# Two-layer encoder trunk: another order of loads, warming products and norm sums at the program's begin

## Chip, cores and metric

The kernel runs on one core of one Trainium2 chip. The metric is the device time of one execution in microseconds (us), lower is better. A number such as L652 is a line of the kernel before. Engines are named as in the profile: PE does the matrix products, ACT and DVE the elementwise work, POOL a few fills, SP issues most of the transfers, and a DMA can also be issued from ACT's queue.

## The reference, cut to what matters

Input x is 512 positions by 1024 channels, in float32. Each of the two layers is this:

```python
hn = rmsnorm(x, norm_mix_g[l])
proj = hn @ w_in[l]
(aq, ak, av, bx, by, cq, ck, cv, dq, dk, dv, gl) = jnp.split(proj, split_points, axis=-1)
ya = mixer_a(aq, ak, av, ...)            # dense attention
yb = mixer_b(bx, by, conv_w[l], ...)     # convolution, two gated scans over time, GeLU gate
yc, yd = mixer_c(cq, ck, cv, ...), mixer_d(dq, dk, dv, ...)   # windowed attentions
merged = sum(gate_i * (y_i @ w_proj_i))
x = x + merged @ w_out[l]
x = x + jnp.square(jax.nn.relu(rmsnorm(x, norm_mlp_g[l]) @ w_mlp1[l])) @ w_mlp2[l]
```

A last rmsnorm follows. rmsnorm scales each position by 1/sqrt(mean of squares + eps). In mixer_b the scan's decay is `a = exp(log_a)` and its input is `sqrt(1 - a*a) * (i * xc)`; r and i are sigmoids of small products of xc, the output of the convolution of bx.

## The kernel before, in words

**Products.** Channels lie on the 128 partitions, positions along the free axis. A float32 product is done as three: every operand is split into a high part (a cast, on ACT) and a low part (a subtraction, on DVE), and PE multiplies high by high, high by low and low by high. Weights come in chunks of 128 by 1024 (eight tiles of 128 columns; `PLAN` lists their order). A chunk is loaded by SP (`wload`, L96), cast by ACT (`whi`, L111, three buffers) and subtracted by DVE (`wlo`, L122); `take` (L147) hands the next one out and casts up to three chunks ahead. The cast of a chunk waits until PE has done with the chunk three places earlier. A group of products over one chunk is 24 products, three for each of eight k.

**The begin.** `setup` (L294) loads the vectors `ve`, fills `ones` on DVE and copies one element of it on ACT. `all` (L1379) issues 16 products of `ones` by `ones`, whose result nobody reads, then loads the eight x tiles and the first chunks on SP. `xg_tile` (L247) makes the high part xh of an x tile times the norm's gain on ACT and the low part xl on DVE; `sumsq` (L255) adds up squares for the norm, whose factor is applied later. Chunks 0 and 1 come in halves.

**Phase 1 of a layer** (`phase1`, L417) runs the 30 groups of `P1SEQ` (L47) in this order; n is the place in it: BX0 and BX1 (n = 0, 1) interleaved by `several`, K0, K1, BX2 (n = 4), AQ, AQ, BX3, BY0 and so on, then pairs of groups for CQ0, CQ1, DQ0, DK0 (n = 20, 21), DQ1 (22, 23), DK1 (24, 25), DQ2, DK2. After each pair `rope` rotates its two results on DVE. `norm_cols` (L264) makes the norm's factor from the squares with eight small products, `rows` and `spread_rows` turn it into a tile `rb` that `conv_b` (L577) and others multiply by.

**The queue of small steps.** The steps of mixer_b are not issued where their data come up but put in a queue `bq`. `conv_b` adds three steps (tap 0 on ACT, taps 1 and 2, tap 3 on DVE) and, for its first two tiles, a split; `gelu_b` three; `gates_b` (L631) does four small groups of three products, one tanh on ACT each (L652), and adds for its tile f: s1 twice (three activations on ACT, L661 to L663), s2 twice (two operations on DVE, L669 and L670), s3 (two square roots on ACT, L675), s4 twice (a product and a scan on DVE, L679 and L681), s5 (two operations on DVE, L685 and L686, then a cast on ACT, L687) and s6 (DVE, L690). After group n as many steps are taken from the queue as `TICKS[n]` (L49) says, fewer if it holds fewer. `gates_b` is called after the groups 16, 18, 24 and 25 for f = 0 to 3. Before its own products it empties the queue as far as it needs to:

```python
while self.bq and (f not in self.xch or (f > 1 and f - 2 not in self.bdone)):
    self.tick(1)
```

where `bdone` gets f in step s6. So `gates_b(3)`, after group 25, takes steps until s6 of f = 1 is out. Engines work in the order of issue.

**Accumulators.** `wide` (L165) hands out accumulator tiles by the tags mm, s and t in turn, two buffers for each tag; a buffer is free again when its last reader in the program is done. Group 24 has tag mm and is read by the rope after group 25. The four tiles of `gates_b(2)` have the tags s, t, mm, s, group 25 has t, and the tiles of `gates_b(3)` have mm, s, t, mm.

Nothing reorders any of this: the program's order is the order on each engine.

Of the kernel before, what the change touches and what calls it, by code (L numbers as in the profile page):

```python
# [11 lines left out]
F32 = mybir.dt.float32  # L12
F32R = mybir.dt.float32r
I32 = mybir.dt.int32
AF = mybir.ActivationFunctionType
ALU = mybir.AluOpType
# [7 lines left out]
KD = DM // 128  # L24
# [17 lines left out]

E1, E2, E3, FN = (2, 5, 2, 16)

WU, P0, P1 = (16, 2, 2)

P1SEQ = [("BX", 0), ("BX", 1), ("K", 0), ("K", 1), ("BX", 2), ("AQ", 0, 0), ("AQ", 0, 1), ("BX", 3), ("BY", 0),  # L47
         ("AQ", 1, 0), ("AQ", 1, 1), ("BY", 1), ("BY", 2), ("BY", 3)] + [k + (z,) for k in QKS for z in range(2)]
# [27 lines left out]
class Body:  # L76
# [19 lines left out]
    def wload(self):  # L96
        i = self.n_load
        if i >= len(self.order):
            return
        raw = self.rawp.tile([128, 1024], F32, tag="raw", name="raw")  # L100
        for s in self.parts(i):
            self.nc.sync.dma_start(out=raw[:, s], in_=self.w[i][:, s])
        self.raws[i] = raw
        self.n_load += 1

    def parts(self, i):

        n = (P0, P1, 1)[min(i, 2)]
        return [slice(p * (1024 // n), (p + 1) * (1024 // n)) for p in range(n)]

    def whi(self):  # L111
        i = self.n_split
        while self.n_load <= i:
            self.wload()
        hi = self.hlp.tile([128, 1024], F32R, tag="whi", name="whi")
        lo = self.hlp.tile([128, 1024], F32R, tag="wlo", name="wlo")
        for s in self.parts(i):
            self.nc.scalar.copy(hi[:, s], self.raws[i][:, s])  # L118
        self.hls[i] = (hi, lo)
        self.n_split += 1  # L120

    def wlo(self):  # L122
        i = self.n_lo
        hi, lo = self.hls[i]
        raw = self.raws.pop(i)
        for s in self.parts(i):
            self.nc.vector.tensor_tensor(out=lo[:, s], in0=raw[:, s], in1=hi[:, s].bitcast(F32), op=ALU.subtract)  # L127
        self.n_lo += 1

    def ahead(self, i):  # L130
# [143 lines left out]
    def rows(self, cols, n, pool):  # L274

        nc, rw = self.nc, self.rw
        nc.vector.tensor_copy(rw[:, :, 0:n].bitcast(F32R), cols)
        nc.vector.tensor_tensor(out=rw[:, :, 32:32 + n], in0=cols, in1=rw[:, :, 0:n], op=ALU.subtract)
        ps = self.misc()
        m = 32 + n  # L280
        for c in range(4):
            nc.tensor.matmul(ps[0:m, c * 128:(c + 1) * 128], rw[:, c, 0:m], self.ident)
        row = pool.tile([m, S], F32R, tag=f"row{n}", name="row", bufs=1)
        nc.scalar.copy(row, ps[0:m, :])
        return row
# [8 lines left out]
    def setup(self):  # L294
        nc = self.nc
        cp = self.cp
        self.cs = cp.tile([128, NC_], F32, name="cs")
        self.ve = cp.tile([128, DEPTH * NV + 8], F32, name="ve")
        self.ones = cp.tile([128, 128], F32, name="ones")
        nc.sync.dma_start(out=self.ve, in_=self.vec)  # L300
        nc.vector.memset(self.ones, 1.0)
        nc.scalar.copy(self.ones[0:1, 0:1], self.ones[0:1, 0:1])
        self.ident = self.cs[:, C_ID:C_ID + 128]
        nl = DEPTH
        self.xh = self.xgp.tile([128, KD, S], F32R, name="xh")
        self.xl = self.xgp.tile([128, KD, S], F32R, name="xl")
        self.acc = cp.tile([128, S], F32, name="acc")
        self.rb = cp.tile([128, S], F32, name="rb")
        self.d_hb = cp.tile([128, nl, 32], F32, name="d_hb")
        self.d_lgb = cp.tile([128, nl, 16], F32, name="d_lgb")  # L310
        self.d_sp = cp.tile([128, nl, 8], F32, name="d_sp")
        self.d_nsp = cp.tile([128, nl, 8], F32, name="d_nsp")
        self.d_nsink = cp.tile([128, nl, 8], F32, name="d_nsink")
# [103 lines left out]
    def phase1(self, l):  # L417
        nc, p1 = self.nc, self.p1
        nv, ns = nc.vector, nc.scalar
# [23 lines left out]
        X, sqt, SUM = {}, {}, {}  # L443
# [3 lines left out]
        def squares(key, Xs, n=128):  # L447

            sqt[key] = []
            for z, x in enumerate(Xs):  # L450
                if z == 0 or n == 128:
                    sq = p1.tile([128, S], F32, tag="sqq", name="sqq", bufs=2)
                    sqt[key].append(sq)
                    o = 0
                else:
                    o = n
                ns.activation(out=sq[o:o + n], in_=x[0:n], func=AF.Square)
# [29 lines left out]


        X["bx", 0], X["bx", 1] = self.several([("BX", f) for f in range(2)], self.xmv, (1, 2, 3, 4, 6))
        rcol = self.rcol = self.norm_cols()  # L490
        nv.tensor_scalar(out=self.rs8, in0=rcol, scalar1=0.125, scalar2=None, op0=ALU.mult)
        nv.tensor_scalar(out=self.nrs8, in0=rcol, scalar1=-0.125, scalar2=None, op0=ALU.mult)
        r2 = self.smt(4, "r2")
        nv.tensor_tensor(out=r2, in0=rcol, in1=rcol, op=ALU.mult)
        X["k", 0] = self.group("K", 0)
        row = self.rows(rows(rcol, 1), 1, p1)
        X["k", 1] = self.group("K", 1)
        ns.copy(self.rb, self.spread_rows(row, 1, 0))
        if l == 0:
            self.derive()  # L500

        rd = self.drp.tile([S], F32, tag="rd", name="rd")
        nc.sync.dma_start(out=rd.rearrange("(c p) -> p c", p=128), in_=rcol)
        nc.sync.dma_start(out=self.roff, in_=rd.rearrange("(p r) -> p r", r=4))
        self.conv_b(l, 0, X["bx", 0])
        self.conv_b(l, 1, X["bx", 1])
        squares("k", (X["k", 0], X["k", 1]), 64)
        X["bx", 2] = self.group("BX", 2)
        self.conv_b(l, 2, X["bx", 2])
        head_sums("k", 2, C_SELK)  # L510
        yk = head_scale("k", 2)
# [867 lines left out]
    def all(self):  # L1379
        nc = self.nc  # L1380
        self.setup()
        self.xs = self.drp.tile([KD, 128, S], F32, tag="xs", name="xs")
        warm = self.misc()
        with self.tc.tile_pool(name="xin", bufs=1) as xin:
            self.sqp = xin
            xt = xin.tile([128, KD, S], F32, name="xt")
            for _ in range(WU):
                nc.tensor.matmul(warm[:, 0:128], self.ones, self.ones)
            xg = lambda c: self.xg_tile(xt[:, c], c, self.v(0, V_GMIX + c))
            for c in range(KD):  # L1390
                nc.sync.dma_start(out=xt[:, c], in_=self.x[c])
                if c in (0, 1, KD - 1):
                    self.wload()
            nc.sync.dma_start(out=self.cs, in_=self.cst)
            for c in range(KD):
                xg(c)
                if c < 2:
                    self.whi()
                    self.lows()
                if c >= 2:  # L1400
                    self.sumsq(xt[:, c - 2], c == 2)
            for c in range(KD - 2, KD):
                self.sumsq(xt[:, c], False)
        for l in range(DEPTH):
            self.layer(l)
# [10 lines left out]
def _pack_weights(i):  # L1416
# [13 lines left out]
    for l in range(DEPTH):  # L1430
# [3 lines left out]
        for key in PLAN:  # L1434
# [36 lines left out]
            else:  # L1471
                c = cols(i["w_mlp2"][l][a[0] * DM:(a[0] + 1) * DM], span(0, a[1]))
            parts.append(np.ascontiguousarray(c).reshape(128, 1024))
    return np.stack(parts)


# [77 lines left out]
```

## Time and profile before

| | before |
|---|---|
| median of 3 runs | 2004.0 us (2003.87 to 2004.54) |
| the profiled execution's own time | 2003.11 us |
| its span in the profile | 2001.3 us |
| PE busy | 1984.2 us, 99% of the span |
| DVE, ACT busy | 1299.9 us (65%), 1000.5 us (50%) |

Times in the profile count from the start of the span. In a timeline a row is: start in us, duration in us, engine, line, operation, written tile <- read tiles, shapes, how many were merged into the row, and in brackets the idle time of the engine before it and what ended it. PEld is the load of weights that goes ahead of a product. A float32 product of `ones` shows as two records.

### The profile page before, as it was taken

To read this page: it belongs to the slowest core of one execution; us is meant where nothing else is said; L and a number is where in the kernel's file an instruction comes from. 1 tells how busy PE (TensorE), PEld (TensorE's weight loads), DVE (VectorE), ACT (ScalarE), POOL (GpSimd) and SP (SyncE) were. 2 spreads that over 40 slices of the span, in tenths; PEclk is the share of its full clock that TensorE was granted. 3 is DMA by queue.
4 is the path that set the end of the run, shared out by engine and by line. 5 is a ranking of instruction groups with operands and counts; after the bars stand their busy time and mean duration, and the time that the engine had idled before them with its cause. 6 is when DMAs were issued, how large, how long until landed. Compare 5 with 4: busy or idle time off the path is not lost.

```text
span 2001.3 us, 25982 instructions
## 1 busy us (share of the span) xinstructions
PE 1984.2 (99%) x9732; PEld 1654.7 (83%) x9732; DVE 1299.9 (65%) x2330; ACT 1000.5 (50%) x1751; POOL 1.7 (0%) x12
## 2 busy tenths in 40 slices
PE   9999999999999999999999999999999999999998
PEld 7888789888888888888888888898877888888887
DVE  6889775766666554444658897758675755544445
ACT  4357786855734332332333668868466344332322
POOL 0000000000000000000000000000000000000000
PEclk9999999999999999999999999999999999999999
DMA  5544415334443223323335553152343423323231
GB/s 194 159 145 141 134 54 154 116 101 116 117 131 131 94 97 95 101 90 104 123 111 169 157 167 97 53 172 93 111 131 95 162 95 105 95 95 103 91 102 64
DMA packets 92910, 233.35 MB, mean 117 GB/s; under 512 B 17496, under 2 KB 23768, under 8 KB 92784
## 3 DMA queue, kind: packets, MB, share of 16 engines
q1 hardware_dynamic: 89904, 227.50, 36.7%
q10 hardware_dynamic: 2880, 4.20, 0.6%
q8 instruction: 77, 1.26, 0.3%
q14 instruction: 49, 0.40, 0.1%
HBM read 207.38 MB, written 24.27 MB: 116 GB/s over the span
## 4 chain that ended last, share of the span: by engine, by line
PE 88%; DVE 7%; ACT 3%; issue 2%; DMA 1%; SPq 0%; DVEq 0%; ACTq 0%
PE ps_mm L177 12%; PE ps_mm L179 12%; PE ps_mm L178 11%; PE ps_t L177 6%; PE ps_t L179 6%; PE ps_t L178 6%; PE ps_s L177 6%; PE ps_s L179 6%; PE ps_s L178 6%; PE ps_o L890 2%; PE ps_t L869 2%; DVE wlo L127 1%; ACT whi L118 1%; PE ps_s L830 1%; PE ps_s L980 1%
## 5 line engine op out<-in xcount | busy, mean ns | idle before, releaser
L118 ACT CAST whi<-raw 128x1024 fp32r<-128x1024 f32 (+1 forms) x318 | 329.0, 1041 | 310.5 <-PE ps_mm L178 99.6
L127 DVE TENSOR_TENSOR wlo<-raw,whi 128x1024 fp32r<-128x1024 f32 (+1 forms) x318 | 384.6, 1213 | 89.5 <-ACT whi L118 86.5
L177 PE MATMUL ps_mm<-xh,whi 128*128 128x512 f32 x720 | 285.9, 397 | 0.2
L179 PE MATMUL ps_mm<-xh,wlo 128*128 128x512 f32 x720 | 281.2, 391 | 1.1 <-DVE wlo L127 1.1
L178 PE MATMUL ps_mm<-xl,whi 128*128 128x512 f32 x720 | 280.9, 390 | 0.0
L179 PEld LDWEIGHTS ps_mm<-xh,wlo 128*128 128x128 f32 x720 | 135.2, 188 | 31.4 <-DVE wlo L127 1.9
L177 PEld LDWEIGHTS ps_mm<-xh,whi 128*128 128x128 f32 x720 | 135.3, 188 | 27.8 <-ACT whi L118 1.1
L178 PEld LDWEIGHTS ps_mm<-xl,whi 128*128 128x128 f32 x720 | 135.4, 188 | 26.2
L177 PE MATMUL ps_t<-xh,whi 128*128 128x512 f32 x368 | 143.8, 391 | 0.0
L179 PE MATMUL ps_t<-xh,wlo 128*128 128x512 f32 x368 | 143.2, 389 | 0.0
L178 PE MATMUL ps_t<-xl,whi 128*128 128x512 f32 x368 | 143.2, 389 | 0.0
L177 PE MATMUL ps_s<-xh,whi 128*128 128x512 f32 x352 | 138.7, 394 | 0.0
L179 PE MATMUL ps_s<-xh,wlo 128*128 128x512 f32 x352 | 137.1, 389 | 0.0
L178 PE MATMUL ps_s<-xl,whi 128*128 128x512 f32 x352 | 137.0, 389 | 0.0
L879 DVE TENSOR_TENSOR PT<-ps_t,PT 128x512 fp32r<-128x512 f32 (+2 forms) x128 | 75.0, 586 | 63.4 <-ACT PT L876 58.9
L863 ACT ACTIVATE P<-P,al 128x512 f32<-128x512 f32 (+2 forms) x128 | 82.7, 646 | 18.9 <-DVE al L862 17.8
L876 ACT CAST PT<-ps_t 128x512 fp32r<-128x512 f32 (+2 forms) x128 | 63.8, 500 | 46.2 <-PE ps_o L890 42.7
L177 PEld LDWEIGHTS ps_t<-xh,whi 128*128 128x128 f32 x368 | 69.1, 188 | 15.1 <-issue 1.0
L179 PEld LDWEIGHTS ps_t<-xh,wlo 128*128 128x128 f32 x368 | 69.1, 188 | 14.5
L178 PEld LDWEIGHTS ps_t<-xl,whi 128*128 128x128 f32 x368 | 69.1, 188 | 14.2
L177 PEld LDWEIGHTS ps_s<-xh,whi 128*128 128x128 f32 x352 | 66.1, 188 | 14.6 <-issue 1.3
L178 PEld LDWEIGHTS ps_s<-xl,whi 128*128 128x128 f32 x352 | 66.1, 188 | 14.0 <-issue 0.5
(434 smaller groups left out, 4184.9 us busy)
## 6 DMA issues: line engine op xcount, KB each, us to landing
raw<-in_w_dram SPq DMA_DIRECT2D x314, 512.0 KB, 3.5
Qr<-qD SPq DMA_DIRECT2D x48, 128.0 KB, 3.9
Kd<-kD SPq DMA_DIRECT2D x48, 128.0 KB, 3.9
qsA<-stk SPq DMA_DIRECT2D x32, 128.0 KB, 2.3
qsC<-stk SPq DMA_DIRECT2D x32, 128.0 KB, 2.5
K<-ks SPq DMA_DIRECT2D x16, 256.0 KB, 8.7
Q<-qsA SPq DMA_DIRECT2D x16, 256.0 KB, 6.3
Q<-qsC SPq DMA_DIRECT2D x16, 256.0 KB, 5.6
```

What stands on the lines that cost most here:

```text
L118: self.nc.scalar.copy(hi[:, s], self.raws[i][:, s])
L127: self.nc.vector.tensor_tensor(out=lo[:, s], in0=raw[:, s], in1=hi[:, s].bitcast(F32), op=ALU.subtract)
L177: mm(ps, sh, mh, start=(k == 0), stop=False)
L178: mm(ps, sh, ml, start=False, stop=False)
L179: mm(ps, sl, mh, start=False, stop=(k == n - 1))
L830: nc.tensor.matmul(ps[:, 0:n], qq, Kt[j][:, 0, b0 * 128:b1 * 128], start=True, stop=False)
L863: ns.activation(out=P[:, 0:n], in_=P[:, 0:n], func=AF.Copy, scale=ls)
L869: nc.tensor.transpose(pt[:, b * 128:(b + 1) * 128], P[:, b * 128:(b + 1) * 128], self.ident)
L876: ns.copy(st["dst"][0], st["src"])
L879: nv.tensor_tensor(out=st["dst"][1], in0=st["src"], in1=st["dst"][0].bitcast(F32), op=ALU.subtract)
L890: nc.tensor.matmul(o, a, b, start=(n_ == 0), stop=(n_ == len(mm) - 1))
L980: nc.tensor.matmul(ps[:, o:o + w], Q[:, q0:q0 + 128], K[:, z, k0:k0 + w], start=(z == 0), stop=(z == 1))
```

## The change

At the begin, the warming products go from 16 to 11 and no longer wait for ACT's copy of an element of `ones` (that copy now has another target and comes later). `ve` is loaded from ACT's queue. Chunks 0 and 1 come in four quarters each: the first quarters from ACT's queue, the others from SP between the x tiles; casts and subtractions of a quarter come after every second x tile. The squares of the x tiles start after the sixth tile in place of the third, and chunk 2 is split before the last five of them.

In phase 1 of both layers, `norm_cols` comes after K0 (before: ahead of it), `rows` after K1 (before: after K0), `spread_rows` and `rb` in the middle of BX2 (before: after K1), the squares of K ahead of BX2, and the `conv_b` of the tiles 0 and 1 after BX2 (before: ahead of it). `P1SEQ`, `TICKS` and `GATES` are as before.

```diff
-WU, P0, P1 = (16, 2, 2)
+WU, P0 = (11, 4)
...
-        raw = self.rawp.tile([128, 1024], F32, tag="raw", name="raw")
-        for s in self.parts(i):
-            self.nc.sync.dma_start(out=raw[:, s], in_=self.w[i][:, s])
-        self.raws[i] = raw
+        raw = self.raws[i] = self.rawp.tile([128, 1024], F32, tag="raw", name="raw")
+        self.nc.sync.dma_start(out=raw, in_=self.w[i])
...
+    def first_loads(self, queue, p):
+
+        s = slice(p * (1024 // P0), (p + 1) * (1024 // P0))
+        for i in range(2):
+            if p == 0:
+                self.raws[i] = self.rawp.tile([128, 1024], F32, tag="raw", name="raw")
+            queue.dma_start(out=self.raws[i][:, s], in_=self.w[i][:, s])
+        self.n_load = 2
+
+    def first_split(self, p):
+        s = slice(p * (1024 // P0), (p + 1) * (1024 // P0))
+        for i in range(2):
+            if p == 0:
+                self.hls[i] = [self.hlp.tile([128, 1024], F32R, tag=t, name=t) for t in ("whi", "wlo")]
+            hi, lo = self.hls[i]
+            self.nc.scalar.copy(hi[:, s], self.raws[i][:, s])
+            self.nc.vector.tensor_tensor(
+                out=lo[:, s], in0=self.raws[i][:, s], in1=hi[:, s].bitcast(F32), op=ALU.subtract
+            )
...
-        nc.sync.dma_start(out=self.ve, in_=self.vec)
+        nc.scalar.dma_start(out=self.ve, in_=self.vec)
         nc.vector.memset(self.ones, 1.0)
-        nc.scalar.copy(self.ones[0:1, 0:1], self.ones[0:1, 0:1])
...
         X["bx", 0], X["bx", 1] = self.several([("BX", f) for f in range(2)], self.xmv, (1, 2, 3, 4, 6))
+        X["k", 0] = self.group("K", 0)
         rcol = self.rcol = self.norm_cols()
...
-        X["k", 0] = self.group("K", 0)
+        X["k", 1] = self.group("K", 1)
         row = self.rows(rows(rcol, 1), 1, p1)
-        X["k", 1] = self.group("K", 1)
-        ns.copy(self.rb, self.spread_rows(row, 1, 0))
         if l == 0:
             self.derive()
...
+        squares("k", (X["k", 0], X["k", 1]), 64)
+        X["bx", 2] = self.group("BX", 2, within=lambda: ns.copy(self.rb, self.spread_rows(row, 1, 0)))
         self.conv_b(l, 0, X["bx", 0])
         self.conv_b(l, 1, X["bx", 1])
-        squares("k", (X["k", 0], X["k", 1]), 64)
-        X["bx", 2] = self.group("BX", 2)
         self.conv_b(l, 2, X["bx", 2])
...
+            load = lambda c: nc.sync.dma_start(out=xt[:, c], in_=self.x[c])
+            load(0)
+            self.first_loads(nc.scalar, 0)
+            nc.scalar.copy(self.d_sp[0:1, 0, 0:1], self.ones[0:1, 0:1])
+            for p in range(P0):
+                if p > 0:
+                    self.first_loads(nc.sync, p)
+                for c in (2 * p + 1, 2 * p + 2):
+                    if c < KD:
+                        load(c)
+            self.wload()
+            nc.sync.dma_start(out=self.cs, in_=self.cst)
             xg = lambda c: self.xg_tile(xt[:, c], c, self.v(0, V_GMIX + c))
             for c in range(KD):
-                nc.sync.dma_start(out=xt[:, c], in_=self.x[c])
-                if c in (0, 1, KD - 1):
-                    self.wload()
-            nc.sync.dma_start(out=self.cs, in_=self.cst)
-            for c in range(KD):
                 xg(c)
-                if c < 2:
-                    self.whi()
-                    self.lows()
-                if c >= 2:
-                    self.sumsq(xt[:, c - 2], c == 2)
-            for c in range(KD - 2, KD):
+                if c % 2 == 0:
+                    self.first_split(c // 2)
+                if c >= 5:
+                    self.sumsq(xt[:, c - 5], c == 5)
+            self.whi()
+            self.lows()
+            for c in range(3, KD):
                 self.sumsq(xt[:, c], False)
```

## Rows read from the trace of the kernel before

**Rows 1.** The page, part 1: busy time, share of the span, instructions of each engine.

```profile
PE 1984.2 (99%) x9732; PEld 1654.7 (83%) x9732; DVE 1299.9 (65%) x2330; ACT 1000.5 (50%) x1751; POOL 1.7 (0%) x12
```

**Rows 2.** Waits of PE: total us, times, longest; the two longest lines of eight.

```profile
PE ps_misc L1388 <- ACT ones L302: 2.3, 1, 2.3
PE ps_s L1340 <- ACT dg L1336: 1.7, 1, 1.7
```

**Rows 3.** Timeline of the begin, all engines.

```profile
0.74 1.28 ACT L302 ACT_TABLE_LOAD   x1 [0.74 <-PEq L1546]
0.84 0.17 DVE L301 MEMSET ones<- 128x128 f32 x1 [0.84 <-PEq L1546]
...
2.28 6.03 PE L1388 MATMUL ps_misc<-ones 128*128 128x128 f32 x32 [2.28 <-ACT ones L302]
...
3.95 0.72 ACT L250 ACTIVATE xh<-xt,ve 128x512 fp32r<-128x512 f32 x1 [1.72 <-DMA xt<-in_x_dram]
...
7.22 0.72 ACT L250 ACTIVATE xh<-xt,ve 128x512 fp32r<-128x512 f32 x1 [0.20 <-DMA xt<-in_x_dram]
...
8.06 0.47 PE L206 MATMUL ps_s<-xh,whi 128*128 128x512 f32 x1
...
19.03 0.39 PE L208 MATMUL ps_t<-xh,wlo 128*128 128x512 f32 x1
```

**Rows 4.** Warming products by stretch: length, PE busy (records), granted clock, DMA share, GB/s.

```profile
2.28:6.28 4.00, 4.00 (x18) 1.00 0.89 283
7.28:7.78 0.50, 0.50 (x7) 1.00 1.05 369
```

**Rows 5.** Timeline of PE, layer 0: gates of tiles 2 and 3.

```profile
159.28 0.39 PE L177 MATMUL ps_s<-xch,whi 128*128 128x512 f32 x1
...
167.44 0.39 PE L177 MATMUL ps_mm<-xch,whi 128*128 128x512 f32 x1
...
169.48 0.39 PE L177 MATMUL ps_mm<-xch,whi 128*128 128x512 f32 x1
```

**Rows 6.** Timeline of ACT in the same stretch.

```profile
148.41 1.06 ACT L118 CAST whi<-raw 128x1024 fp32r<-128x1024 f32 x1 [0.18 <-ACT whi L118]
...
151.30 0.82 ACT L661 ACTIVATE btq<-btg,d_sp 128x512 f32<-128x512 f32 x1
...
156.53 1.28 ACT L675 ACT_TABLE_LOAD   x1
...
161.02 0.63 ACT L675 ACTIVATE btq<-btq 128x512 f32<-128x512 f32 x1 [2.56 <-DVE btq L669]
...
163.90 0.69 ACT L652 ACTIVATE btg<-ps_s,d_lgb 128x512 f32<-128x512 f32 x1
...
167.92 0.62 ACT L687 CAST yB<-btq 128x512 fp32r<-128x512 f32 x1 [1.59 <-DVE btq L686]
168.44 0.68 ACT L652 ACTIVATE btg<-ps_mm,d_lgb 128x512 f32<-128x512 f32 x1
```

**Rows 7.** Timeline of DVE in the same stretch.

```profile
158.34 2.04 DVE L378 TENSOR_TENSOR stkf<-tt 128x512 f32<-128x512 f32 x2
160.30 0.68 DVE L669 SCALAR_TENSOR_TENSOR btq<-btg,btq 128x512 f32<-128x512 f32 x1
...
162.22 1.22 DVE L681 TENSOR_TENSOR_SCAN btq<-bta,btg 128x512 f32<-128x512 f32 x1
163.37 1.20 DVE L127 TENSOR_TENSOR wlo<-raw,whi 128x1024 fp32r<-128x1024 f32 x1
...
167.19 0.69 DVE L686 SCALAR_TENSOR_TENSOR btq<-btq,yb 128x512 f32<-128x512 f32 x1
```

**Rows 8.** Timeline of ACT and PE, layer 1, the same place.

```profile
1157.41 0.62 ACT L687 CAST yB<-btq 128x512 fp32r<-128x512 f32 x1 [1.58 <-DVE btq L686]
1157.94 0.68 ACT L652 ACTIVATE btg<-ps_mm,d_lgb 128x512 f32<-128x512 f32 x1
...
1158.98 0.39 PE L177 MATMUL ps_mm<-xch,whi 128*128 128x512 f32 x1
```

More of the change, by code (lines that the diff above doesn't have):

```diff
@@ L99, in wload @@
             return
-        raw = self.rawp.tile([128, 1024], F32, tag="raw", name="raw")
-        for s in self.parts(i):
-            self.nc.sync.dma_start(out=raw[:, s], in_=self.w[i][:, s])
-        self.raws[i] = raw
+        raw = self.raws[i] = self.rawp.tile([128, 1024], F32, tag="raw", name="raw")
+        self.nc.sync.dma_start(out=raw, in_=self.w[i])
         self.n_load += 1
-    def parts(self, i):
-        n = (P0, P1, 1)[min(i, 2)]
-        return [slice(p * (1024 // n), (p + 1) * (1024 // n)) for p in range(n)]
+    def first_loads(self, queue, p):
[15 more added lines that the diff above has]
+            )
+        if p == P0 - 1:
+            self.n_split = self.n_lo = 2
+            del self.raws[0], self.raws[1]
     def whi(self):
@@ L116, in whi @@
         lo = self.hlp.tile([128, 1024], F32R, tag="wlo", name="wlo")
-        for s in self.parts(i):
-            self.nc.scalar.copy(hi[:, s], self.raws[i][:, s])
+        self.nc.scalar.copy(hi, self.raws[i])
         self.hls[i] = (hi, lo)
@@ L125, in wlo @@
         raw = self.raws.pop(i)
-        for s in self.parts(i):
-            self.nc.vector.tensor_tensor(out=lo[:, s], in0=raw[:, s], in1=hi[:, s].bitcast(F32), op=ALU.subtract)
+        self.nc.vector.tensor_tensor(out=lo, in0=raw, in1=hi.bitcast(F32), op=ALU.subtract)
         self.n_lo += 1
```

## Prediction

> **What bounds the kernel now.** I read four views: the page's busy times, PE's waits, the timeline of the begin, and the timelines of PE, ACT and DVE where the moved code ends up. PE is busy 99% of the span [rows 1], so a part of this change counts only where PE stands still, now or afterwards. The waits of PE name one long stop, 2.3 us before the first warming product; no other reaches 2 us [rows 2]. In the timeline of the begin the reader sees two blocks: the warming products keep PE until the first real product at 8.06, and the pair BX0 and BX1 then runs to its last product at 19.03 [rows 3], which leaves PE at 19.26. The third place is the gates of tiles 2 and 3: nine products go from 167.44 to 169.48 without a gap [rows 5], 0.227 us each, the price of a real product from here on.
>
> **The change, part by part.**
>
> *Warming.* Today PE waits for ACT's copy, behind a table load of 1.28; afterwards it waits for the fill of `ones` alone, done at 1.01 [rows 3], so it starts at 1.06 in place of 2.28. Eleven products are 22 records. At the start 18 records take 4.0 us, 0.22 each; later seven take 0.5 [rows 4], so the clock is then at the upper of its two levels (1.2 and 2.4 GHz), though the granted clock reads 1.00 in both rows. 22 at 0.22 are 4.8: PE is free at 5.9.
>
> *First operands.* xh of tile 0 can start at 3.95 as today at the latest: `ve` and x0 are now issued side by side, x0 first on SP. 3.95 + 0.72 gives 4.67; the quarter's cast lies between a quarter of 1.06 [rows 6] and the whole; I take 0.4, as a row has fixed cost too, so 5.1. On DVE xl ends at 5.45 (4.70 + 0.75, sized as xh) and the quarter's low part at 5.9 (0.45, against 1.20 for a whole chunk [rows 7]). So the operands stand when the warming ends. The pair's 48 products at 0.227 take 10.9 and end at 16.8 in place of 19.26: 2.45 gained. Two things eat into it: x1 lands somewhere between 5.0 and today's 7.2 [rows 3], which can hold the second k by up to 0.6; and if the clock rises at today's moment (about 7.0) rather than after as much work, some 1.1 us run at half pace, 0.6 lost. I take 2.2, between 1.3 and 2.6. The quarters, the two issues on ACT's queue ahead of its first work and the later squares cost PE nothing beyond this: the squares are wanted only after K0, 5.4 us later than today, which hides them; without that cover their five casts and additions would cost about 3.
>
> *Norm and `rb` one group later.* The same products and transfers in another order: 0. K0 hides the squares, K1 the factor's chain of small DVE operations, half of BX2 the row's cast, as one group did for each before. The stores of the factor keep their place on SP, ahead of loads wanted several groups later. Bounds: 0 to 0.5 for each layer.
>
> *The queue of steps.* This part is easily missed. After BX2 (n = 4) two steps are taken from the queue. Today it holds the eight of the first two `conv_b`; afterwards these come later and it is empty, so nothing is taken. Nothing makes up for this: counting `TICKS` by hand, the queue stays two steps behind until `gates_b(3)` empties it after group 25. Today s2, s3 and s4 of f = 1 are out after group 24, and after group 25 the other s4, s5, s6. Afterwards s1, s2, s2 are out after group 24, and *s3, both s4, s5 and s6 all* come between group 25 and the gates of tile 3, in both layers.
>
> Who waits for that? ACT is in order. The tanh of the first gate product of tile 3 stands behind s5's cast: 167.92, then the tanh 168.44 to 169.12 [rows 6]. The fourth gate product of tile 3 needs the same accumulator buffer (mm has two, and group 24 holds one until the rope), so it waits for that tanh. It starts at 169.48 [rows 5]: a slack of 0.36. Layer 1 is the same: tanh at 1157.94, product at 1158.98 [rows 8].
>
> Now the chain after the change, in the times of the trace before, from the end of group 22 when a cast starts at 148.41 [rows 6]: cast 1.05, its low part 1.2, s4 of f = 0 (product and scan) 1.95, s5's two operations 1.4, its cast 0.65, the cast of split 3 0.5, a table load 1.3: 156.5. s1's three activations (first one 0.82 [rows 6]) about 2.1, a chunk's cast 1.0, its low part 1.2, the rope's last pair 2.04, four operations of s2 2.4, a low part 1.15: DVE is free at 166.2 (durations of its steps as in [rows 7]). ACT meanwhile does the other s1 (161.6), a cast (162.5), the four tanh of tile 2 at 0.57 (164.8), a table load of 1.28 and the root (0.63): 166.75. From there two s4 at 1.9, s5 1.4, its cast 0.65, a table load back to tanh 1.3, the tanh 0.69: 174.6. PE wants it at 169.48: **a stop of 5.0 us in each layer**, with nothing behind it to run, as PE is in order too. From below: even with DVE free, the roots follow the tanh of tile 2 on ACT, and these follow products that end at 162.0 (159.28 and twelve at 0.227 [rows 5]): 162.85 + 1.28 + 0.63 + 7.8 for the rest of the chain is 172.6, a stop of 3.1. From above: one more low part in DVE's way, 6.2. What goes in exchange: DVE is 1 us less behind PE afterwards, up to 0.5 for each layer.
>
> *Sum.* 2003.11 (the profiled execution; its span is 2001.3) - 2.2 + 2 x 5.0 = 2010.9. The median of the runs lies 0.9 higher, so 2011.8.
>
> **The rivals.** (1) *The stops also cost the clock.* After five idle microseconds PE may come back at its lower level. No row shows an idle time in the middle longer than 1.7 [rows 2], so the trace neither supports nor excludes it. The price by the start: 22 records took 4.8 there that take 2.4 later, so 2.3 for each layer in which it happens: 2014.1 or 2016.4. The Trainium skill ("TensorE: Matmul & The Clock Gate", Part 1, HAM oscillation) says that the clock is throttled again when bursts of products have idle gaps that are long enough; by that rule, this rival holds. Chance 0.30. (2) *No stop: the other side.* The place is the same buffer of tag mm. If the tanh of tile 3 is out within 0.36 of today, because DVE and ACT catch up before group 25 or the buffer is free otherwise, only the begin counts: 2001.8. It decides at one point, s5's cast done by 168.3 in today's times. For it: DVE and ACT have idle time in both layers, such as the 2.56 before a root and the 1.59 before the cast [rows 6]. Against it: those waits are for DVE, which has no gap from 158.34 to the cast [rows 7], and the lower bound above. Chance 0.15. (3) *The begin doesn't do what it says*: x1 and the quarters share the transfers' rate and come as late as now, the pair ends at 19.2, the stops stay: 2014.0. For it: DMA share 0.89 and 1.05 [rows 4]. Against: half the bytes are wanted for the first k. Chance 0.08.
>
> **How the numbers follow.** The forecast, stops without the clock, has 0.47: from 2004.0 - 2.6 + 6.2 - 1.0 = 2006.6 to 2004.0 - 1.3 + 12.4 = 2015.1. The range is 2007.0 to 2016.5: it takes in rivals (1) and (3) and leaves out (2). A measurement of this kernel can tell about 0.2%, 4 us, from no change. Slower by more: the forecast but for 0.03 that falls under 2008, (1) and (3), 0.82. Within: that 0.03 and most of (2), 0.15. Faster: 0.03, a begin that gains over 4 us without stops.
>
> **What would show it.** Right: PE's waits have a line for ps_mm behind a tanh of L652 with two stops of about 5; a table load between s5's cast and that tanh; two roots behind the tanh of tile 2; 22 warming records from 1.06 and a first real product near 5.9; the pair's end near 17. Wrong: the gates of tile 3 without a gap, or a first product after 7.

## The result and the profile after

The changed kernel takes 2017.9 us (median of 5 runs, 2017.48 to 2020.0) against 2004.0: ratio 1.0071, 95% interval 1.006 to 1.0082. It is slower, as forecast, but lies above the range (2007.0 to 2016.5). The profiled execution took 2019.35 us, its span is 2017.6; the one of before took 2003.11. So the two traces differ by 16.2 where the medians differ by 13.9. The begin and the time at the low clock, below, differ from one profile to the next; how much of these 2.3 us they make is not shown.

Page, part 1, and waits of PE (total us, times, longest), the changed kernel; compare [rows 1, 2]:

```profile
PE 1989.4 (99%) x9722; PEld 1656.9 (82%) x9722; DVE 1301.7 (65%) x2334; ACT 1001.2 (50%) x1755; POOL 1.7 (0%) x12
...
PE ps_mm L191 <- ACT btg L664: 12.7, 2, 6.4
...
PE ps_misc L1400 <- DVE ones L315: 1.1, 1, 1.1
```

The wait before the warming fell from 2.3 to 1.1. A new line stands on top: two waits, 12.7 us together, for a tanh of the gates. And PE is busy 5.2 us longer with ten records fewer: something made its products slower (five warming products fewer account for the ten records).

Timeline of PE around the stop in layer 0, the changed kernel (start, duration, ..., idle before it); compare [rows 5]:

```profile
168.28 0.39 PE L193 MATMUL ps_t<-xch,wlo 128*128 128x512 f32 x1
175.02 0.79 PE L191 MATMUL ps_mm<-xch,whi 128*128 128x512 f32 x1 [6.35 <-ACT btg L664]
175.61 0.63 PE L192 MATMUL ps_mm<-xch,whi 128*128 128x512 f32 x1
...
180.73 0.43 PE L192 MATMUL ps_s<-xl,whi 128*128 128x512 f32 x1
181.00 0.40 PE L193 MATMUL ps_s<-xh,wlo 128*128 128x512 f32 x1
```

Windows of PE in the same place (length, PE busy and records, granted clock, DMA share, GB/s):

```profile
160.00:168.60 8.60, 8.60 (x39) 1.00 0.49 131
168.60:175.00 6.40, 0.06 (x1) 0.92 0.21 74
175.00:180.80 5.80, 5.78 (x14) 0.50 0.00 0
180.80:187.00 6.20, 6.20 (x29) 1.00 0.49 126
```

After the stop the products start 0.43 apart in place of 0.23, and the granted clock reads 0.50: the lower of the two levels (1.2 GHz). Thirteen products run so. Layer 1 is the same: a stop of 6.33, then seven products at the lower level.

ACT and DVE ahead of it, the changed kernel; compare [rows 6, 7]. To set a time of this trace beside one of the trace before, add 1.0 to 1.1, by which PE runs ahead here:

```profile
147.40 1.06 ACT L133 CAST whi<-raw 128x1024 fp32r<-128x1024 f32 x1 [4.38 <-PE ps_s L192]
154.16 0.62 ACT L699 CAST yB<-btq 128x512 fp32r<-128x512 f32 x1 [5.71 <-DVE btq L698]
...
165.11 1.28 ACT L687 ACT_TABLE_LOAD   x1
166.40 1.15 ACT L687 ACTIVATE btq<-btq 128x512 f32<-128x512 f32 x2
172.35 0.62 ACT L699 CAST yB<-btq 128x512 fp32r<-128x512 f32 x1 [4.79 <-DVE btq L698]
172.98 1.28 ACT L664 ACT_TABLE_LOAD   x1
174.28 0.69 ACT L664 ACTIVATE btg<-ps_mm,d_lgb 128x512 f32<-128x512 f32 x1
```

```profile
148.39 1.29 DVE L391 TENSOR_TENSOR stkf<-tt 128x512 f32<-128x512 f32 x2
149.60 1.22 DVE L141 TENSOR_TENSOR wlo<-raw,whi 128x1024 fp32r<-128x1024 f32 x1
150.73 0.69 DVE L691 TENSOR_TENSOR btg<-btq,btg 128x512 f32<-128x512 f32 x1
...
167.07 0.69 DVE L691 TENSOR_TENSOR btg<-btq,btg 128x512 f32<-128x512 f32 x1 [0.52 <-ACT btq L687]
```

Here is the forecast order: the tanh of tile 2, a table load, two roots, on DVE two s4 and s5, then s5's cast, a table load back, and only then the tanh that frees PE's buffer.

The begin, the changed kernel; compare [rows 3]:

```profile
1.06 5.07 PE L1400 MATMUL ps_misc<-ones 128*128 128x128 f32 x22 [1.06 <-DVE ones L315]
...
5.06 0.41 ACT L119 CAST whi<-raw 128x256 fp32r<-128x256 f32 x1 [0.45 <-DMA raw<-in_w_dram]
...
5.78 0.77 PE L220 MATMUL ps_s<-xh,whi 128*128 128x512 f32 x1
...
6.90 0.41 ACT L119 CAST whi<-raw 128x256 fp32r<-128x256 f32 x1 [1.43 <-DMA raw<-in_w_dram]
...
7.36 0.50 PE L220 MATMUL ps_t<-xh,whi 128*128 128x512 f32 x1 [0.21 <-ACT whi L119]
...
8.78 0.50 PE L221 MATMUL ps_s<-xl,whi 128*128 128x512 f32 x1 [0.21 <-DVE xl L265]
...
18.24 0.39 PE L191 MATMUL ps_mm<-xh,whi 128*128 128x512 f32 x1
```

The first product comes at 5.78, but the first of BX1 only at 7.36, when the first quarter of chunk 1 has landed (6.90) and is cast. PE is free of the pair at 18.24, against 19.26: 1.0 gained.

Where the time went: the start of the same product in two timelines of PE, less its start in the kernel before (worked out from the rows of each trace; us).

| product, time before | after | e2: lag alone | e4: filler | e1: in step | e5 |
|---|---|---|---|---|---|
| first of the head sums, layer 0, 38.38 | -1.07 | +0.61 | -1.05 | -0.07 | -1.70 |
| fourth gate product of tile 3, 169.48 | +5.54 | +7.23 | +5.57 | -0.07 | -1.70 |
| first with xh as the moving side, 191.92 | +8.39 | +9.67 | +5.70 | -0.07 | -1.70 |
| first of the dense attention's output, 229.11 | +7.54 | +8.83 | +5.70 | -0.05 | -1.66 |
| head sums, layer 1, 1027.88 | +8.65 | +9.32 | +6.13 | -0.12 | -1.57 |
| fourth gate product of tile 3, 1158.98 | +15.24 | +15.95 | +12.75 | -0.12 | -1.57 |
| first with xh as the moving side, 1181.42 | +16.91 | +17.66 | +12.88 | -0.12 | -1.57 |
| first of the dense attention's output, 1218.63 | +16.08 | +16.79 | +12.88 | -0.11 | -1.57 |
| last, 1994.16 | +16.18 | +16.83 | +12.92 | +0.32 | -1.53 |

Down the column "after": the begin -1.07; the stops +6.61 and +6.59; the clock behind them +2.85 and +1.67; -0.85 and -0.83 come back ahead of the attention; 1.1 more is lost in layer 0 between 229 and 600 of the kernel before. Together with 0.1 behind the last of these rows that is the 16.2.

### The profile page after: what moved, and what is told of

Its sections match the earlier page's. It is cut to its first block, busy times and chain, and to the rows that moved or that the text cites. A ratio compares the mean times of both kernels' runs of the same rounds, so it can differ in the third digit from the quotient of the medians.

```text
span 2017.6 us, 25985 instructions
## 1 busy us (share of the span) xinstructions
PE 1989.4 (99%) x9722; PEld 1656.9 (82%) x9722; DVE 1301.7 (65%) x2334; ACT 1001.2 (50%) x1755; POOL 1.7 (0%) x12
## 4 chain that ended last, share of the span: by engine, by line
PE 87%; DVE 6%; ACT 4%; issue 1%; DMA 1%; SPq 0%; ACTq 0%; DVEq 0%
PE ps_mm L191 12%; PE ps_mm L193 11%; PE ps_mm L192 11%; PE ps_s L191 6%; PE ps_s L193 6%; PE ps_s L192 6%; PE ps_t L191 6%; PE ps_t L192 6%; PE ps_t L193 6%; PE ps_o L902 2%; PE ps_t L881 2%; ACT whi L133 1%; PE ps_s L842 1%; PE ps_s L992 1%; PE ps_mm L203 1%
## 5 line engine op out<-in xcount | busy, mean ns | idle before, releaser
L133 ACT CAST whi<-raw 128x1024 fp32r<-128x1024 f32 x314 | 327.1, 1047 | 344.9 <-PE ps_mm L192 119.1
L141 DVE TENSOR_TENSOR wlo<-raw,whi 128x1024 fp32r<-128x1024 f32 x314 | 382.3, 1221 | 95.9 <-ACT whi L133 92.9
L193 PEld LDWEIGHTS ps_s<-xh,wlo 128*128 128x128 f32 x352 | 66.7, 190 | 14.7 <-DVE wlo L141 0.4
```

The source lines that it names most:

```text
L133: self.nc.scalar.copy(hi, self.raws[i])
L141: self.nc.vector.tensor_tensor(out=lo, in0=raw, in1=hi.bitcast(F32), op=ALU.subtract)
L193: mm(ps, sl, mh, start=False, stop=(k == n - 1))
```

## The experiments

A ratio here is taken against runs of the kernel before made beside the experiment (medians 2003.8 to 2004.0). Where only the profile of an experiment is read, it is one execution.

**e1: the two missing steps.** The changed kernel with

```diff
         self.conv_b(l, 1, X["bx", 1])
+        self.tick(2)
```

> The changed kernel with two steps of the queue taken right behind the first two conv_b, so that the queue stands as in the kernel before from there on. Theory (the lag of two steps makes both stops and the clock loss): no stop at the fourth gate product of tile 3 in either layer, granted clock 1.00 throughout, and the time falls by 2 x (6.35 + 2.9) = 18.5 from the profiled 2019.35, to about 2001 with the profile and 2002.5 to 2003.5 in the median: some 1 us below the kernel before. Rival (the later norm and squares cost something of their own, the lag is only part): stops of over 1 us stay, 2006 or more.

Measured: 2002.66 us median of 11 runs, ratio 0.9994 (0.9985 to 1.0003). Both stops are gone, and with them the low clock; the column e1 is flat from 38.38 to 1218.63. The lag makes the whole loss. The begin of the profiled run (2003.58) gained nothing (-0.07). The other runs have no trace; they spread over 2001.5 to 2003.9, and the profiled one is among the longer.

**e2: the lag alone,** in the kernel before:

```diff
-TICKS = [0, 0, 2, 1, 2, 2, 0, 1,
+TICKS = [0, 0, 2, 1, 0, 2, 0, 1,
```

> The kernel before with one number changed: no step taken after group 4 (TICKS[4] 0 for 2). Nothing else of the change is in it. Theory: the same two stops, each 5.5 (6.35 less the 0.8 by which PE came earlier there), and the clock behind each, 2.9: 2004.0 + 16.8 = 2020.8. Rival (the stops come from the reordered begin, or from DVE being late by the squares): within 2 us of 2004.

Measured: 2019.63 us, ratio 1.008 (1.0066 to 1.0094). Waits of PE in e2:

```profile
PE ps_mm L177 <- ACT btg L652: 12.7, 2, 6.4
PE ps_misc L1388 <- ACT ones L302: 2.3, 1, 2.3
```

One number does it all, with the old begin and the old norm. The stop is as long as in the changed kernel, not 5.5: the chain hangs on a cast that itself waits for PE, so an earlier PE brings the chain along. The cast starts at 149.09 in e2 and at 147.40 in the changed kernel, the stopped product at 176.71 and 175.02: 1.69 apart both times.

**e4: is it the idle time that costs the clock?** The changed kernel, with work that nobody reads in the stop:

```diff
+                if (f, d, gate) == (3, 1, 1):
+                    fill = self.misc()
+                    for _ in range(24):
+                        nc.tensor.matmul(fill[:, 0:128], self.ones, self.ones)
                 ps = self.wide()
```

> The changed kernel with 24 products of ones by ones, which nobody reads, between the third and the fourth gate product of tile 3: 24 x 0.21 = 5.1 us of PE work in a stop of 6.35. The queue still lags. Theory (the clock falls because PE stands idle): the wait for the tanh ends as before, PE is idle for some 1.2 us only, the granted clock stays at 1.00 and the products behind the stop take 0.227 each, so 2 x 2.9 = 5.8 is saved: 2012.1. Rival (the lower clock has another cause, such as the transfers or the other engines at that moment): products of 0.43 behind the stop all the same, 2018.

Timeline of PE, and windows, e4:

```profile
168.52 5.52 PE L660 MATMUL ps_misc<-ones 128*128 128x128 f32 x48
175.05 0.50 PE L191 MATMUL ps_mm<-xch,whi 128*128 128x512 f32 x1 [1.01 <-ACT btg L668]
175.38 0.40 PE L192 MATMUL ps_mm<-xch,whi 128*128 128x512 f32 x1
```

```profile
175.00:180.80 5.80, 5.75 (x25) 1.00 0.00 0
```

The product behind the stop starts at 175.05 as before (175.02), but the clock stays up: 25 records in the window where the changed kernel has 14. So it is PE's idling, not the transfers nor the other engines. The time is 2015.57, only 2.3 below 2017.9 in place of the 5.8 expected. The column e4 tells why: the table's clock steps shrink to 0.13 each, 2.7 and 1.5 less, but the 0.85 that came back in each layer does not: the wait for a chunk's low part at 210.91 of the kernel before (0.53) is absent in the changed kernel and back in e4's layer 0. That DVE got ahead while PE was slow is the likely reason; in layer 1 of e4 a wait of 0.93 in which the profile shows no releaser takes the place of that wait. So the clock's net price for a stop is 1.2 by the medians, and 1.6 by the profiles, of which 0.3 lies in the loss between 229 and 600 (1.1 in the changed kernel, 0.4 in e4).

**e6: one step in place of two.**

```diff
         self.conv_b(l, 1, X["bx", 1])
+        self.tick(1)
```

> The changed kernel with one step in place of two taken behind the first two conv_b, so the queue lags by one. By the order of the queue the roots of f = 1 come after group 24 again and only one s4 more than in e1 lies between group 25 and the gates of tile 3. Theory: the cast of s5 is 1.9 later than in step, the slack is 0.36, so a stop of 1.5 (1.0 to 2.5) in each layer; if a stop that short leaves the clock up, e1's 2002.7 + 3.0 = 2005.7; if the clock falls after it as after 6.35, 2.7 more for each: 2011. Rival (the length of the stop doesn't follow the number of steps): a stop of 5 or more as with two.

Measured: 2014.46 us, ratio 1.0054 (1.004 to 1.0067): neither. ACT and PE in e6:

```profile
163.47 0.63 ACT L688 ACTIVATE btq<-btq 128x512 f32<-128x512 f32 x1 [2.55 <-DVE btq L682]
164.67 0.63 ACT L688 ACTIVATE btq<-btq 128x512 f32<-128x512 f32 x1 [0.57 <-DVE btq L682]
...
166.26 1.28 ACT L665 ACT_TABLE_LOAD   x1
167.56 0.69 ACT L665 ACTIVATE btg<-ps_s,d_lgb 128x512 f32<-128x512 f32 x1
```

```profile
169.46 0.80 PE L191 MATMUL ps_mm<-xch,whi 128*128 128x512 f32 x1 [3.06 <-ACT btg L665]
170.05 0.63 PE L192 MATMUL ps_mm<-xch,whi 128*128 128x512 f32 x1
...
173.95 0.50 PE L191 MATMUL ps_mm<-xch,whi 128*128 128x512 f32 x1 [0.80 <-ACT btg L665]
```

The stop comes earlier and in two. With one step of lag both s2 pairs stand behind the rope's last pair on DVE (the rope at 160.79, s2 at 162.74 and 163.94; before, the first pair was out at 153.61). So the roots start only at 163.47 and 164.67, and ACT has them, as before, *ahead* of the tanh of tile 2. That tanh comes at 167.56, and the *first* gate product of tile 3 waits 3.06 for the third of them; then the clock is down for some six products, and the fourth waits 0.80 more. The expectation counted only the steps behind group 25 and missed what the shift did to the tanh of tile 2.

**e8: another buffer.** The changed kernel; the fourth gate product takes a buffer that is free.

```diff
-                ps = self.wide()
+                ps = self.wide() if (f, d, gate) != (3, 1, 1) else self.ps("s")
+                self.rr += (f, d, gate) == (3, 1, 1)
```

> The changed kernel, lag and all, in which the fourth gate product of tile 3 takes a buffer of tag s, whose last reader (the fourth tanh of tile 2) is long done, in place of the one of tag mm. Theory (the late tanh is the bound and the buffer only the place where PE meets it): the fourth gate product runs without a wait, and the next group, DQ2, whose accumulator has tag s too, waits for the second tanh of tile 3, 0.58 later than the first: the stop moves three products on and is 6.35 - 0.68 + 0.58 = 6.25 long, the clock falls as before, total within 1 us of the changed kernel's 2017.9. Rival (the shared buffer is the cause, another one removes the stop): 2003 or less.

Measured: 2017.91 us, ratio 1.0069 (1.0055 to 1.0082), the changed kernel's time. PE in e8:

```profile
175.14 0.80 PE L191 MATMUL ps_s<-xh,whi 128*128 128x512 f32 x1 [6.27 <-ACT btg L665]
```

The stop moved three products on, to the next group, 6.27 long. The shared buffer is where PE meets the late tanh, not why it is late.

**e7: the new order alone,** with the old begin: `phase1` as in e1, all else as before.

> The begin of the kernel before (16 warming products, halves, one queue, squares from the third tile) with the new order of phase 1 and the two steps taken behind the first two conv_b. Theory (the later norm and rb cost nothing once the queue is in step): 2004.0 within 1 us. Rival (the later norm helps or hurts by itself, by the waits of K1 and BX2 for DVE and ACT): more than 1.5 us to either side.

Measured: 2004.92 us, ratio 1.0006 (0.9997 to 1.0014): 0.9 above the 2004.0 of the expectation, so just inside it, and 1.1 above the 2003.82 of the runs beside it; the interval takes in 1, so it is not told apart from the kernel before. One wait in its profile belongs to the order:

```profile
20.71 0.50 PE L179 MATMUL ps_mm<-xh,wlo 128*128 128x512 f32 x1 [0.42 <-DVE wlo L127]
```

K0 now starts right behind the pair, and the low part of chunk 2, on DVE behind the last squares, is late by 0.42. Behind the pair's last product, the first head sums come 20.0 later here, 19.35 later in the kernel before. The changed kernel splits chunk 2 ahead of the last five squares and has no such wait (19.29).

**e3: the new begin alone,** with phase 1 in the order of the kernel before, `norm_cols` right behind the pair.

> The new begin with the order of phase 1 of the kernel before: norm_cols right behind the pair BX0 and BX1, conv_b ahead of BX2, no lag. Theory (the later norm is there only to cover the squares): the pair ends near 18.0, but the sums of squares stand on DVE only at about 21.5, so PE waits 3 to 3.5 for them in layer 0 and nowhere in layer 1; no stop at the gates: 2004.0 - 1.0 + 3.3 = 2006.3, up to 2009 if the clock falls in that wait. Rival (the squares are done in time anyway): 2003.

Measured: 2008.46 us, ratio 1.0022 (1.0013 to 1.003). PE in e3:

```profile
20.92 1.83 PE L283 MATMUL ps_misc<-ones,acc 128*128 128x1 f32 x8 [2.80 <-DVE acc L276]
22.61 0.78 PE L191 MATMUL ps_mm<-xh,whi 128*128 128x512 f32 x1
23.18 0.63 PE L192 MATMUL ps_mm<-xl,whi 128*128 128x512 f32 x1
```

PE waits 2.80 for the sums, and the products behind are 0.43 apart again (granted clock 0.51 from 22.6 to 27.6). So the later norm is what the later squares need. The clock came down within this stop of 2.80 (granted 1.00 up to 20.5, 0.50 from 20.9), the case for which the expectation had said up to 2009.

**e5: the first quarters side by side,** with e1's two steps:

```diff
-            queue.dma_start(out=self.raws[i][:, s], in_=self.w[i][:, s])
+            (queue if i else self.nc.sync).dma_start(out=self.raws[i][:, s], in_=self.w[i][:, s])
```

> The changed kernel with the two steps taken (as in e1) and with the first quarter of chunk 0 issued on SP right behind x0, that of chunk 1 on ACT's queue right behind ve; nothing else moves. Theory (the begin gained only 0 to 1.1 us because the first quarter of chunk 1 lands at 6.9 to 7.9, eighth and last of the transfers issued at first): it lands near where the first quarter of chunk 0 lands now, 5.1 to 5.6, the first product of group BX1 starts by 6.3 in place of 7.36 (profile of the changed kernel), K0 starts near 17.3 in place of 18.24, and the median is about 1 us below e1, 2001.7. Rival (all the first transfers share one rate, so the order only moves the wait to x1): K0 at 18 or later, within 0.5 of e1.

Measured: 2001.33 us, ratio 0.9988 (0.9979 to 0.9996): faster than both kernels. It is 1.3 below e1 by the medians; ten of its eleven runs are shorter than e1's median, though the intervals of the two ratios overlap. Timeline of ACT and PE, e5:

```profile
4.54 0.71 ACT L119 CAST whi<-raw 128x256 fp32r<-128x256 f32 x2
6.62 1.40 ACT L264 ACTIVATE xh<-xt,ve 128x512 fp32r<-128x512 f32 x2 [1.37 <-DMA xt<-in_x_dram]
```

```profile
6.59 0.39 PE L220 MATMUL ps_t<-xh,whi 128*128 128x512 f32 x1
...
8.18 0.50 PE L221 MATMUL ps_s<-xl,whi 128*128 128x512 f32 x1 [0.29 <-DVE xl L265]
...
17.61 0.39 PE L191 MATMUL ps_mm<-xh,whi 128*128 128x512 f32 x1
```

Both first quarters are cast without a wait for either, BX1 starts at 6.59, K0 at 17.61 (17.3 expected; 17.79 to 19.25 in the five profiles of the changed order of phase 1 with the first quarters on one queue). Now x1 is last, landing at 6.62.

**e9: x1 by the other queue,** on top of e5:

```diff
             self.first_loads(nc.scalar, 0)
+            nc.scalar.dma_start(out=xt[:, 1], in_=self.x[1])
...
-                    if c < KD:
+                    if 1 < c < KD:
```

> The kernel of e5 with x1 issued on ACT's queue behind the quarter of chunk 1, not on SP. In e5 the high part of x1 starts when x1 lands, at 6.62, and the second k waits for it. Theory (the first transfers share one rate, some 876 KB have to land up to x1 whatever queue they take): x1 lands between 6.2 and 7.0, K0 within 0.4 of e5's 17.61, the median within 0.5 of 2001.3. Rival (SP's queue is the narrow one, two queues side by side are faster): x1 by 5.8, K0 by 17.0, 2000.7.

Measured: 2002.67 us, ratio 0.9993 (0.9984 to 1.0002): neither. Timeline of ACT, e9:

```profile
7.20 1.34 ACT L264 ACTIVATE xh<-xt,ve 128x512 fp32r<-128x512 f32 x2 [1.94 <-DMA xt<-in_x_dram]
```

x1 lands at 7.20, 0.6 later than behind two transfers on SP's queue. The pair's last product comes 0.57 later too: it starts 10.75 behind the high part of x1 here, 10.76 in e5. By the medians 1.3 are lost, with intervals that overlap. x2 now stands on SP's queue where x1 stood; that it took x1's share is likely, but no run shows it alone.

## Why the prediction was wrong

The sign, the place and the mechanism of the stops were right: the lag of two steps, both layers, the tanh of tile 3, the line of ps_mm with two stops. One term was put at nothing, the clock, and two sizes were off, all to the same side. In the two profiles: the clock 4.5 for 0, the stops 13.2 for 10.0, the begin 1.1 gained for 2.2. Against that 1.7 came back ahead of the attention, which the sum didn't hold, and 1.1 more was lost in layer 0.

**The clock.** "The forecast, stops without the clock" was the choice that failed; rival (1), 0.30, is what happened. Its price, 2.3 for each layer, was near the 2.85 and 1.67 measured. No row of before spoke for or against it, as the text said; the rule of the Trainium skill that stood beside it ("TensorE: Matmul & The Clock Gate", Part 1, HAM oscillation) did, and the granted clock of 0.50 agrees. When only a rule bears on a case and nothing on the other side, it should have weighed more than 0.30. That rival's own number with both layers, 2016.4, is 1.5 below the result, in part by luck, as its stops were too short and its begin too good, and nothing came back. The top of the range, 2016.5, was this rival with the stop as forecast; with the working's own upper bound of 6.2 for the stop it would have been 2018.8.

**The stop,** 5.0 forecast, 6.2 the upper bound: 6.35 measured, and the product 6.6 later than before. The chain began with "cast 1.05, its low part 1.2, s4 of f = 0": in the trace after, two operations of the rope (148.39, 1.29) stand between the cast and its low part, so the cast of s5 for f = 0 comes at 154.16, that is 155.2 in the times before (1.0 is to be added), for 154.0. The rest of the chain kept some 1.2 of it: the tanh that frees the buffer ends at 174.97, about 176.0 in the times before, for 174.6. The rope's last pair was counted, but only the second one, behind s1. The bound from above allowed for one more low part, also 1.2, and was nearly right. Three slips in the working changed nothing: the listed durations of DVE add up to 166.4, not 166.2, and ACT's 166.75 ruled; s5's cast had to begin by 168.3, not to be done; and the 2.4 for 22 records at the upper level is half of 4.8, where the row that it leans on (seven in 0.5) would give 1.6. The 48 records of e4 in 5.52 give 2.5.

**The begin,** 2.2 forecast (1.3 to 2.6): 1.0 in the profile after, 0.1 to 1.5 over the five profiles with this begin and the later norm (after, e1, e4, e6, e8; at the head sums). Warming (22 records from 1.06, real products at 5.78 for 5.9) and the first quarter of chunk 0 (a cast of 0.41 for 0.4) were right. The step that failed is "the quarters ... cost PE nothing beyond this": the working followed chunk 0 and never asked when the quarter of *chunk 1* lands, third on ACT's queue while three x tiles go by SP. Six profiles have this order of transfers: in e8, e3, e6, after, e4 and e1 the cast of that quarter waits for its landing and starts at 6.50, 6.66, 6.81, 6.90, 6.96 and 7.94, and the pair's last product starts 11.06 to 11.12 behind it each time. So the landing of this one transfer sets the end of the pair. In e1's profile it came so late that K0 started at 19.25, as rival (3) had said. When e5 moved it, x1 became the bound.

**What held.** The later norm costs nothing in the changed kernel: from the pair's last product to the first head sums it takes 19.29 in layer 0, 19.35 before, and from 229.11 to 1027.88, where the norm of layer 1 lies, the column e1 moves by 0.07. The squares need it (e3). Rival (2), no stop, is out. Rival (3) was half right: the begin gained, but less. What came back for the relief of DVE, "up to 0.5 for each layer", was more, 0.85.

## What to carry to other kernels

Where small steps are taken from a queue by a hand-made count, moving the code that *fills* the queue past one count shifts all that follows: count what each call pops, not only what it costs; here two steps were 15 us. Here stops of PE of 2.80 to 6.35 us cost their length and then products at the lower clock; waits of 1.01 (e4) and 1.53 (e5, granted clock 1.00 behind it) cost their length alone. For a begin bound by transfers, list the landing of *every* operand of the first two groups, and issue in the order of use.

## What the hardware showed that was not expected

The moment at which the clock rises at the begin varied: with warming from 1.06 in both, the first real products still start 0.57 apart at 5.78 in the profile after, while in e1's eleven products take 4.12 in place of 5.07 and end by 5.2. The granted clock reads 1.00 in both, so at the begin the level is to be read from the spacing of the records. Stops of 2.80 (e3), 3.06 (e6) and 6.35 us brought the clock down, waits of 1.01 (e4) and 1.53 (e5) did not. Stops of one length did not cost the same: the time at the lower level afterwards was 6.0 and 3.4 us in the two stops of one execution. The granted clock of short stretches shows when it fell. In layer 0 it reads 1.00 from 173.0 to 173.5, 0.97 from there to 174.0 and 0.50 from 174.0 to 175.0, so the clock fell only some 5 us into the stop; in layer 1 it reads 0.50 from 1171.0 on, 3 us into the stop. In layer 1 of e6 it fell when PE was at work again: 1.00 from 1164.6 to 1165.5, behind a stop of 3.05, and 0.51 from 1165.6 to 1172.0. This may be a good part of the spread from 2017.5 to 2020.0, which no trace shows.

Of the 1.1 us lost between 229 and 600 in the changed kernel (0.4 in e4, none in e1), 0.8 lies at 573.4 to 573.9 of the kernel before, where products wait for yD. DVE makes yD late there: it waits 1.13 for a transfer (wb, at 577.61 of the trace after; 0.60 in e4, no such wait in before and e1). Why that transfer is late was not followed up.
